# A hybrid decoder step on one core: score matmuls of the previous tile placed behind the second projection slab of a tile instead of behind the first

## The chip, the cores and the metric

The kernel runs on one core of one Trainium2 chip. The metric is the device time of one execution in microseconds (us), the median of several runs. Five engines run their own instruction streams side by side, each in its own order, and wait for each other by semaphores: TensorE (PE: matmuls and transposes), VectorE (DVE), ScalarE (ACT), GpSimd (POOL) and SyncE (SP), which here issues most of the DMA transfers. The profile gives waits of TensorE under the name of what released it.

## The reference

One layer of a decoder trunk is computed for a prompt of 2048 tokens and for 8 sample sequences of 4 tokens, with width 1024. Cut to what matters here:

```python
h = layer_norm(x) * (1 + scale(c)) + shift(c)          # adaLN: modulated by a vector c per sequence
z, xBC, dt, q, k, v = split(h @ w_in)                  # one combined projection
y_ssm = ssd_scan(silu(causal_conv(xBC)), dt, ...)      # Mamba-2 heads
q, k = rotary(q), rotary(k)                            # first quarter of each head of 64
y_att = softmax([q k^T / 8 in a window of 128, sink]) v   # 8 query heads, 2 key heads
x = layer_norm(alpha * x + gate * (concat(y_ssm, y_att) @ w_out))
x = layer_norm(alpha * x + gate * mlp(modulated x))    # squared ReLU, 4096 wide
```

Outputs are the two y, the convolution and SSM states, and the rotated keys and the values. The change lies in the part that makes q, k, v, dt and the attention of the prompt, all in float32 accuracy: each projection is done as three matmuls of split operands (high x high, high x low, low x high).

## The kernel before

The prompt is 16 tiles of 128 tokens; the 32 sample tokens are a 17th tile, NTILE, worked on after tile 8. The first stretch of the program ("sweep 1", up to about 395 us) loops over the tiles (L767 on). A second sweep for the other columns, the output projection and the MLP follow.

For a tile t the parts are: `st_x` loads x and makes its statistics on DVE (L189, L190) and normalises it (L321). `st_hT` transposes it on TensorE (L330, called xT below), modulates it (DVE L351, POOL L352) and splits it into high and low parts (ACT L171, POOL L172). `st_slab(t, n)` computes one half of 776 projected columns, 24 matmuls of 128x388 (L175 to L177) into one PSUM tile: slab 0 gives dt and most of q, slab 1 the rest of q, k and v. Slab 1 is copied out by ACT (L378, L379) and rotated by DVE (L385 to L388, from whose result kd, L413, is doubled). `st_qkT` transposes q and k (L418, L422) and splits them (qh and kTh on ACT, ql and kTl on DVE). `st_score` does 24 score matmuls (L440, two at a time on two halves of the rows), copies them out on ACT and DVE (L448, L449; the S copies) and runs softmax: maximum (L395), its scaled negative nm (L397), eight exponentials with a sum (L401), reciprocal (L404), and the division on POOL (L405). `st_PT` transposes the result (L464), copied by ACT (L465) and masked by DVE (PC, L467), and `st_PV` multiplies with v (L474), copied out as ao (L479).

In the first nine iterations an "extra" computes one chunk of the modulation for later layers: 8 matmuls (L267), a copy "part" on ACT (L270), one matmul that sums it (L272, the chunk's sum), and an addition on DVE (L274). The chunk's weights and bias are loaded by SP, and the load of a later x stands behind that of the bias in SP's order.

In the last iterations the weights of the second sweep are loaded and split: Wx, the pages pg, and at the end wzst (L634, 2 MB in two loads, into the buffer that tile 15's projection frees; eight splits on ACT with DVE and POOL). `decays_a` is a chain of small DVE operations on dt of all tiles (dkw, ea; L560 to L574).

The order of instructions on each engine isn't that of the source alone. A scheduler takes the source order and a model of its own of how long things take, and places each instruction; only SP's order is written out up to the tenth iteration. An explicit order without a semaphore ties the scores of a tile to a matmul of a projection slab: `mid`, the last matmul of the fourth of its eight steps (k == 3, L372, L373), which `st_score` hands to `side_by_side`, so that no score matmul is put ahead of it. PSUM tiles rotate over three buffers for mm (both slabs, one score tile in four, the chunk), two for tr (all transposes) and three for sc (the other score tiles and PV).

Of the kernel before, what the change touches and what calls it, by code (L numbers as in the profile page):

```python
# [119 lines left out]
def body(tc, I, O):  # L120
# [10 lines left out]
    def mm_tile():  # L131
        return ps.tile([128, 512], F32, tag="mm", name="mm", bufs=3)

    def tr_tile():
        return ps.tile([128, 512], F32, tag="tr", name="tr", bufs=2)
# [14 lines left out]
    def mm_dec(tmp, w, hs, wt):  # L150
        acc = mm_tile()
        for k in range(8):
            for l in range(2):
                PE.matmul(acc[:2 * ND, :w], lhsT=hs(k), rhs=wt(k, l), start=k + l == 0, stop=k + l == 8)
        S.activation(tmp[:2 * ND, :w], acc[:2 * ND, :w], AF.Copy)
        return tmp

    def sum2(out, tmp, w):
        PE.matmul(out[:ND, :w], lhsT=idt[:2 * ND, 192:224], rhs=tmp[:2 * ND, :w], start=True, stop=True)
# [14 lines left out]
    def mm3(out, ahi, alo, bhi, blo, first=True, last=True):  # L174
        PE.matmul(out, lhsT=ahi, rhs=bhi, start=first, stop=False)  # L175
        PE.matmul(out, lhsT=ahi, rhs=blo, start=False, stop=False)  # L176
        return PE.matmul(out, lhsT=alo, rhs=bhi, start=False, stop=last)  # L177
# [18 lines left out]
    def ptok(t):  # L196
        return 128 if t < NTILE else ND
# [114 lines left out]
    def st_x(t):  # L312
        P = ptok(t)
        x = xbuf()
        D.dma_start(out=x[:P], in_=I["x"][128 * t:128 * t + P])
        mv = p1.tile([128, 2], F32, tag="mv", name="mv", bufs=2)
        ln_stats(p1, x, P, mv)
        rs = rstd_of(p1, mv[:P, 1:2], P)
        V.tensor_copy(mean_all[:P, t, 0:1], mv[:P, 0:1])
        V.tensor_copy(mean_all[:P, t, 1:2], rs[:P])  # L320
        V.tensor_scalar(x[:P], x[:P], mv[:P, 0:1], rs[:P], ALU.subtract, ALU.mult)  # L321
        tl["x", t] = x
# [10 lines left out]
    def hT_store(t):  # L333
        hh = tl["hT", t]
        if t < NTILE:
            D.dma_start(out=hT_d[t], in_=hh.bitcast(F32))
        else:
            D.dma_start(out=hT_d[t][:, 0, :, :2 * ND], in_=hh[:, 0, :, :2 * ND].bitcast(F32))
# [17 lines left out]
    def st_slab(t, n):  # L356
        P = ptok(t)
        hh = tl["hT", t]
        if n == 0:
            tl["qkv", t] = p1.tile([128, 648], F32, tag="qkv", name="qkv", bufs=2)  # L360
            tl["v", t] = p1.tile([128, 128], F32, tag="v", name="v", bufs=5)
        qkv = tl["qkv", t]
        mm = tl.pop(("sm", t, n)) if t < 3 else mm_tile()
        sl = slice(388 * n, 388 * n + 388)
        if t == NTILE:
            tmp = mm_dec(p1.tile([128, 512], F32, tag="ao", name="tmp", bufs=2), 388, lambda k: hh[:, 0, k, :2 * ND],
                         lambda k, l: (W1l if l else W1h)[k][:, sl])
            sum2(mm, tmp, 388)
        elif t > 2:
            for k in range(8):  # L370
                ins = mm3(mm[:P, :388], hh[:, 0, k, :P], hh[:, 1, k, :P], W1h[k][:, sl], W1l[k][:, sl], k == 0, k == 7)
                if n == 0 and k == 3:  # L372
                    tl["mid"] = ins  # L373
        if n == 0:
            S.activation(qkv[:P, sl], mm[:P, :388], AF.Copy)
            V.tensor_copy(dt_all[:P, t, :], qkv[:P, 0:8])
            return
        S.activation(qkv[:P, 388:648], mm[:P, 0:260], AF.Copy)  # L378
        S.activation(tl["v", t][:P], mm[:P, 260:388], AF.Copy)  # L379
        qk = qkv[:P, 8:648].rearrange("p (h d) -> p h d", h=10)  # L380
        cos = cc(C_COS + 16 * t, 16)[:P].unsqueeze(1).to_broadcast([P, 10, 16])
        sin = cc(C_SIN + 16 * t, 16)[:P].unsqueeze(1).to_broadcast([P, 10, 16])
        t1 = p1.tile([128, 10, 16], F32, tag="rt1", name="rt1", bufs=1)
        t2 = p1.tile([128, 10, 16], F32, tag="rt2", name="rt2", bufs=1)
        V.tensor_tensor(t1[:P], qk[:, :, 0:16], cos, ALU.mult)  # L385
        V.tensor_tensor(t2[:P], qk[:, :, 0:16], sin, ALU.mult)
        V.tensor_tensor(qk[:, :, 0:8], t1[:P, :, 0:8], t2[:P, :, 8:16], ALU.add)
        V.tensor_tensor(qk[:, :, 8:16], t1[:P, :, 8:16], t2[:P, :, 0:8], ALU.add)  # L388
# [64 lines left out]
    def st_PT(t):  # L453
        Sx = tl.pop(("S", t))
        PT = p1.tile([128, 2, 512], F32, tag="PT", name="PT", bufs=1)
        v = tl["v", t]
        if t > 0:
            PC = p1.tile([128, 2, 512], F32, tag="PC", name="PC", bufs=1)
            vd = p1.tile([128, 128], F32, tag="vd", name="vd", bufs=2)
            V.tensor_tensor(vd, v, tl["v", t - 1], ALU.subtract)  # L460
        for g in range(2):
            tr = tr_tile()
            for r in range(4):
                PE.transpose(tr[:, 128 * r:128 * r + 128], Sx[:, 4 * g + r, :], ident)  # L464
            S.activation(PT[:, g, :], tr, AF.Copy)  # L465
            if t > 0:
                V.tensor_tensor(PC[:, g, :].rearrange("p (r n) -> p r n", r=4), tr.rearrange("p (r n) -> p r n", r=4),  # L467
                                le.unsqueeze(1).to_broadcast([128, 4, 128]), ALU.mult)
        tl["PT", t] = [(v, PT)] if t == 0 else [(tl["v", t - 1], PT), (vd, PC)]

    def st_PV(t):
        terms = tl.pop(("PT", t))
        o = sc_tile()
        side_by_side([lambda i=i, vv=vv, pt=pt, g=g: PE.matmul(  # L474
            o[64 * g:64 * g + 64, :], lhsT=vv[:, 64 * g:64 * g + 64], rhs=pt[:, g, :], start=i == 0,
            stop=i == len(terms) - 1, tile_position=(0, 64 * g))
            for i, (vv, pt) in enumerate(terms) for g in (1, 0)])
        ao = p1.tile([128, 4, 128], F32, tag="ao", name="ao", bufs=2)
        S.activation(ao.rearrange("p r n -> p (r n)"), o, AF.Copy)  # L479
        S.dma_start(out=att_d[t], in_=ao)  # L480
# [219 lines left out]
    n = len(seq)  # L700
# [66 lines left out]
    for i in range(n + 3):  # L767
        if i == 10:
            start.close()
        g = lambda j: seq[j] if 0 <= j < n else None  # L770
        t = g(i)
        if g(i + 5) is not None:
            st_x(g(i + 5))
        if i == 0:
            hT_store(2)
        elif i > 1 and g(i + 1) is not None:
            hT_store(g(i + 1))
        if t is not None:
            st_slab(t, 0)
        if g(i - 2) is not None and g(i - 2) < NTILE:  # L780
            st_PT(g(i - 2))
        if g(i - 1) is not None and g(i - 1) < NTILE:
            st_score(g(i - 1))
        if t is not None:
            st_slab(t, 1)
        if i >= 1 and extras:
            extras.pop(0)()
        if g(i - 2) is not None and g(i - 2) < NTILE:
            st_PV(g(i - 2))
        if t is not None and t < NTILE:  # L790
            st_qkT(t)
        if (i == 0 or i > 2) and g(i + 3 + 2 * (i == 0)) is not None:
            st_hT(g(i + 3 + 2 * (i == 0)))
        if t == NTILE:
            extras += [lambda: (dec_qT(), dec_score(0)), lambda: (dec_PT(0), dec_PV(0), dec_score(1)),
                       lambda: (dec_PT(1), dec_PV(1))]
        if i == 13:
            for j in range(2):
                w2_raw(j, wb0[:, j])
        if i == 14:  # L800
            for j in range(2):
                w2_raw(2 + j, hbuf[:, j])
        if i == 15:
            for j in range(2):
                w2_raw(6 + j, xb1[:, j])
            for k in range(2):
                w2_load(k)
            xq = pb.tile([128, 1024], F32, tag="xq", name="xq")
        if i == n - 1:
            ld_hT(0)  # L810
            for k in range(2, NA):
                w2_load(k)
            for j in range(2):
                w2_raw(4 + j, hbuf[:, j])
            decays_a()
            wz_raw()
        if i == n:
            for k in range(4, 8):
                w2_load(k)
            xproj(0, range(4))  # L820
            for k in range(4):
                wz_load(k)
        if i == n + 1:
            xproj(0, range(4, 8))
            for k in range(4, 8):
                wz_load(k)
            decays_b()
# [719 lines left out]
```

## Time and profile before

| what | value |
|---|---|
| median of 3 runs (lowest, highest) | 2451.91 us (2450.31, 2454.03) |
| the profiled execution | 2451.32 us, span 2449.5 us |
| TensorE busy | 2373.8 us, 97% of the span |
| DVE, ACT, POOL busy | 1445.4, 768.5, 859.9 us |
| mean granted TensorE clock | 0.989 |

The span runs from the first to the last instruction; 1.8 us of the execution lie outside. A row of a timeline has the start, the duration, the engine, the source line, the operation with the tiles it writes and reads, and in brackets the idle time ahead of it with the instruction that ended it. The line of a helper stands for all its callers (L171 and L172 for every split, L175 to L177 for every projection), so there the tile's name tells which it is: hb is the split input of sweep 1, hT that of the second sweep.

### The profile page before, as it was taken

What the parts mean: (1) busy time and instruction counts of PE and PEld (TensorE: products, weight loads), DVE (VectorE), ACT (ScalarE), POOL (GpSimd) and SP (SyncE); (2) the same over time, 40 slices, a digit from 0 to 9 for tenths busy, and PEclk for the clock granted to TensorE, in tenths of its full rate; (3) what the DMA queues carried; (4) which work ended last, traced back from release to release, by engine and by line L of the source; (5) the groups of instructions that cost most, each with busy time, mean ns of one, the idle gap of its engine ahead of it and who ended that gap; (6) DMA issues with size and microseconds to landing.
All of it is one profiled execution on the core that took longest, in us unless ns stands there. A gap on an engine that the chain in (4) does not pass through costs nothing.

```text
span 2449.5 us, 32265 instructions
## 1 busy us (share of the span) xinstructions
PE 2373.8 (97%) x12695; PEld 1987.6 (81%) x12695; DVE 1445.4 (59%) x2533; ACT 768.5 (31%) x1568; POOL 859.9 (35%) x587
## 2 busy tenths in 40 slices
PE   8899989999999999999999999999999999999997
PEld 6566769977997887887888888888889889889885
DVE  6766667877788766355454443448454554443448
ACT  3545554333343545412212212123312212212221
POOL 4333531233223223533323324337333323323335
PEclk9999999999999999999999999999999999999998
DMA  8755333223324356222112211117211211111111
GB/s 314 258 196 169 122 121 96 75 74 109 104 95 151 129 181 234 84 69 65 61 60 72 63 35 61 43 54 217 64 57 45 67 52 52 66 38 35 50 41 71
DMA packets 116104, 242.11 MB, mean 99 GB/s; under 512 B 26080, under 2 KB 61360, under 8 KB 112800
## 3 DMA queue, kind: packets, MB, share of 16 engines
q1 hardware_dynamic: 111552, 230.07, 28.1%
q10 hardware_dynamic: 4400, 9.98, 1.1%
q8 instruction: 100, 1.64, 0.3%
q14 instruction: 52, 0.43, 0.1%
HBM read 185.66 MB, written 55.37 MB: 98 GB/s over the span
## 4 chain that ended last, share of the span: by engine, by line
PE 80%; DVE 7%; ACT 1%; issue 1%; POOL 1%; DMA 1%; POOLq 0%; ACTq 0%; DVEq 0%; SPq 0%
PE sc L175 11%; PE sc L177 11%; PE sc L176 11%; PE mm L175 11%; PE mm L177 11%; PE mm L176 11%; PE tr L175 2%; PE tr L177 2%; PE tr L176 2%; DVE xc L667 1%; PE tr L1298 1%; PE sc L932 1%; PE sc L1129 1%; DVE nb L1325 0%; DVE p L1313 0%
## 5 line engine op out<-in xcount | busy, mean ns | idle before, releaser
L172 POOL TENSOR_TENSOR wdl<-st,wdh 128x1024 fp32r<-128x1024 f32 x63 | 154.6, 2455 | 480.7 <-ACT wdh L171 480.7
L1283 DVE TENSOR_TENSOR r<-r 128x320 f32<-128x320 f32 (+1 forms) x160 | 131.2, 820 | 303.0 <-ACT A L1279 103.1
L1313 DVE TENSOR_TENSOR p<-mm,p 128x512 f32<-128x512 f32 x278 | 187.8, 686 | 123.2 <-PE mm L177 123.2
L171 ACT ACTIVATE wdh<-st 128x1024 fp32r<-128x1024 f32 x63 | 66.9, 1061 | 557.1 <-PE mm L177 173.2
L175 PE MATMUL sc<-H,wvh 128*128 128x352 f32 (+1 forms) x640 | 225.7, 353 | 5.3 <-ACT r L1277 5.3
L176 PE MATMUL sc<-H,wvh 128*128 128x352 f32 (+1 forms) x640 | 226.0, 353 | 0.0
L177 PE MATMUL sc<-H,wvl 128*128 128x352 f32 (+1 forms) x640 | 225.7, 353 | 0.0
L175 PE MATMUL sc<-H,wuh 128*128 128x352 f32 (+1 forms) x640 | 223.8, 350 | 0.0
L177 PE MATMUL sc<-H,wul 128*128 128x352 f32 (+1 forms) x640 | 223.1, 349 | 0.0
L176 PE MATMUL sc<-H,wuh 128*128 128x352 f32 (+1 forms) x640 | 222.9, 348 | 0.0
L1277 ACT ACTIVATE r<-sc 128x352 f32<-128x352 f32 (+1 forms) x160 | 81.6, 511 | 291.7 <-PE sc L177 281.5
L1151 DVE TENSOR_TENSOR st<-st,gf 128x1024 f32<-128x1024 f32 x64 | 108.8, 1701 | 95.1 <-POOL wdl L172 65.7
L175 PEld LDWEIGHTS sc<-H,wvh 128*128 128x128 f32 x640 | 120.8, 189 | 18.1 <-ACT r L1277 5.7
L176 PEld LDWEIGHTS sc<-H,wvh 128*128 128x128 f32 x640 | 120.7, 189 | 12.3
L177 PEld LDWEIGHTS sc<-H,wvl 128*128 128x128 f32 x640 | 120.7, 189 | 11.9
L175 PEld LDWEIGHTS sc<-H,wuh 128*128 128x128 f32 x640 | 120.1, 188 | 11.1 <-ACT r L1277 0.8
L177 PEld LDWEIGHTS sc<-H,wul 128*128 128x128 f32 x640 | 120.5, 188 | 10.2
L176 PEld LDWEIGHTS sc<-H,wuh 128*128 128x128 f32 x640 | 120.2, 188 | 10.0
L183 POOL TENSOR_TENSOR rs<-ve,mhalf 128x1 f32<-128x1 f32 (+2 forms) x68 | 48.3, 710 | 210.2 <-DVE ve L182 187.9
L667 DVE SCALAR_TENSOR_TENSOR xc<-xq,cvw,xc 128x256 f32<-128x256 f32 x192 | 103.6, 543 | 3.3
L1282 DVE TENSOR_TENSOR ud<-r 128x32 f32<-128x32 f32 x32 | 48.2, 1506 | 92.2 <-ACT r L1277 92.2
L172 POOL TENSOR_TENSOR wvl<-st,wvh 128x1024 fp32r<-128x1024 f32 x32 | 77.1, 2410 | 63.9 <-ACT wvh L171 60.8
(496 smaller groups left out, 6521.0 us busy)
## 6 DMA issues: line engine op xcount, KB each, us to landing
st<-in_wd SPq DMA_DIRECT2D x64, 512.0 KB
st<-in_wu SPq DMA_DIRECT2D x63, 512.0 KB
wa<-in_w_ada SPq DMA_DIRECT2D x32, 512.0 KB
hT_d<-hb SPq DMA_DIRECT2D x16, 1024.0 KB
hT<-hT_d SPq DMA_DIRECT2D x16, 512.0 KB
hT<-hT_d SPq DMA_DIRECT2D x8, 1024.0 KB
csb<-cs_d SPq DMA_DIRECT2D x16, 512.0 KB
st<-xhat_d SPq DMA_DIRECT2D x16, 512.0 KB
```

What stands on the lines that cost most here:

```text
L171: S.activation(hi, src, AF.Copy)
L172: (eng or V).tensor_tensor(lo, src, hi.bitcast(F32), ALU.subtract)
L175: PE.matmul(out, lhsT=ahi, rhs=bhi, start=first, stop=False)
L176: PE.matmul(out, lhsT=ahi, rhs=blo, start=False, stop=False)
L177: return PE.matmul(out, lhsT=alo, rhs=bhi, start=False, stop=last)
L183: G.tensor_tensor(r[:P], v[:P], mhalf[:P, 0:n], ALU.pow)
L667: V.scalar_tensor_tensor(dst_, src(j), cvw[:, f, j:j + 1], dst_, ALU.mult, ALU.add)
L1151: V.tensor_tensor(st, raw, scale, ALU.mult)
L1277: S.activation(r[:, :n], mm[:, :n], AF.Relu)
L1282: V.tensor_tensor(ud, r[:, w:n], r[:, w:n], ALU.mult)
L1283: V.tensor_tensor(r[:, :w], r[:, :w], r[:, :w], ALU.mult)
L1313: V.tensor_tensor(acc[t][:, sl], mm, acc[t][:, sl], ALU.add)
```

## The change

The anchor `mid` moves from the first slab to the second, and in the loop the second slab of a tile comes ahead of the scores of the tile before.

```diff
@@ -369,7 +369,7 @@
         elif t > 2:
             for k in range(8):
                 ins = mm3(mm[:P, :388], hh[:, 0, k, :P], hh[:, 1, k, :P], W1h[k][:, sl], W1l[k][:, sl], k == 0, k == 7)
-                if n == 0 and k == 3:
+                if n == 1 and k == 3:
                     tl["mid"] = ins
         if n == 0:
             S.activation(qkv[:P, sl], mm[:P, :388], AF.Copy)
@@ -779,10 +779,10 @@
             st_slab(t, 0)
         if g(i - 2) is not None and g(i - 2) < NTILE:
             st_PT(g(i - 2))
+        if t is not None:
+            st_slab(t, 1)
         if g(i - 1) is not None and g(i - 1) < NTILE:
             st_score(g(i - 1))
-        if t is not None:
-            st_slab(t, 1)
         if i >= 1 and extras:
             extras.pop(0)()
         if g(i - 2) is not None and g(i - 2) < NTILE:
```

The instructions stay the same in number and size. On every engine the order is unchanged up to the first slab of tile 3 (about 90 us) and from the second sweep's projections on (about 395 us). In between it is new; three places show it.

TensorE at tile 6, before (146 to 166 us in the profile; the first row is the end of slab 0, the L175 and L177 rows behind it are the begin and end of slab 1):

```order
L177 MATMUL mm<-pg_128,hb_104 128x388
L330 MATMUL tr<-idt,hbuf 128x128 x4
L440 MATMUL sc<-kTh,qh 128x256
L330 MATMUL tr<-idt,hbuf 128x128 x4
...
L440 MATMUL sc<-kTh,ql 128x256
L175 MATMUL mm<-pg_121,hb_104 128x388
...
L464 MATMUL tr<-idt,S 128x128 x4
...
L177 MATMUL mm<-pg_128,hb_104 128x388
L267 MATMUL mm<-wa,scT 32x512 x8
L474 MATMUL sc<-PT,v 64x512 x2
L474 MATMUL sc<-PC,vd 64x512 x2
L272 MATMUL mm<-part,idt 9x512
```

and in the change, from the xT transposes inside slab 0 on:

```order
L330 MATMUL tr<-idt,hbuf 128x128 x8
...
L464 MATMUL tr<-idt,S 128x128 x8
...
L177 MATMUL mm<-pg_128,hb_104 128x388
L440 MATMUL sc<-kTh,qh 128x256 x2
...
L440 MATMUL sc<-kTh,ql 128x256
L267 MATMUL mm<-wa,scT 32x512 x8
L418 MATMUL tr<-idt,qkv 128x128 x4
L422 MATMUL tr<-idt,kd 128x128 x2
L474 MATMUL sc<-PT,v 64x512 x2
L474 MATMUL sc<-PC,vd 64x512 x2
L272 MATMUL mm<-part,idt 9x512
```

The scores of tile 5 now follow slab 1 of tile 6 in one run, the transposes of softmax (of tile 4) stand together inside slab 1, and q and k of tile 6 are transposed ahead of the chunk's sum.

ScalarE at the same tile, before:

```order
L448 ACTIVATE S<-sc 128x256
L171 ACTIVATE hb_101<-hbuf 128x512
L465 ACTIVATE PT<-tr 128x512 x2
L401 ACTIVATE S,su<-S,nm 128x128
L399 ACTIVATE ex<-ex 128x8
L401 ACTIVATE S,su<-S,nm 128x128 x7
L378 ACTIVATE qkv<-mm 128x260
L379 ACTIVATE v<-mm 128x128
L270 ACTIVATE part<-mm 128x512
```

and in the change:

```order
L465 ACTIVATE PT<-tr 128x512 x2
L378 ACTIVATE qkv<-mm 128x260
L379 ACTIVATE v<-mm 128x128
L448 ACTIVATE S<-sc 128x256 x2
L448 ACTIVATE S<-mm 128x256
L448 ACTIVATE S<-sc 128x256
L270 ACTIVATE part<-mm 128x512
L171 ACTIVATE qh<-tr 128x512
L171 ACTIVATE kTh<-tr 128x2x128
L401 ACTIVATE S,su<-S,nm 128x128
```

Part, qh and kTh have moved from behind the eight exponentials to ahead of them.

ScalarE at the end of the stretch, where tile 15 is done (pg_4130 to pg_4309 are the eight wzst pages), before:

```order
L562 ACTIVATE dkw_3871<-dkw_3871 128x136
L171 ACTIVATE pg_4130<-wzst 128x512
L401 ACTIVATE S,su<-S,nm 128x128
L399 ACTIVATE ex<-ex 128x8
L401 ACTIVATE S,su<-S,nm 128x128 x7
L171 ACTIVATE qh<-tr 128x512
L171 ACTIVATE kTh<-tr 128x2x128
L171 ACTIVATE pg_4133<-wzst 128x512
```

and in the change:

```order
L171 ACTIVATE pg_4130<-wzst 128x512
...
L171 ACTIVATE pg_4309<-wzst 128x512
L171 ACTIVATE qh<-tr 128x512
L479 ACTIVATE ao<-sc 128x512
L561 ACTIVATE dkw_3871<-dt_all 128x136
L171 ACTIVATE kTh<-tr 128x2x128
L480 DMA att_d<-ao 128x512
L562 ACTIVATE dkw_3871<-dkw_3871 128x136
L401 ACTIVATE S,su<-S,nm 128x128
```

All eight splits of wzst now stand ahead of qh and kTh of tile 15, and the exponentials (of tile 14) behind them.

## The prediction, made before the result was known

> **What bounds the kernel now.** I read the page first, then the waits of TensorE between 60 and 400 us (the only stretch in which the order differs), then the timeline around each long wait.
>
> ```profile
> span 2449.5 us, 32265 instructions
> PE 2373.8 (97%) x12695; PEld 1987.6 (81%) x12695; DVE 1445.4 (59%) x2533; ACT 768.5 (31%) x1568; POOL 859.9 (35%) x587
> ```
>
> TensorE is busy for 2373.8 of 2449.5 us. The change adds and removes no matmul, so it can win or lose only a part of the 75.7 us in which TensorE stands idle, the matmuls slowed by a lower clock behind such an idle, and the switches between kinds of matmul. The profiled execution took 2451.32 us, 1.8 more than its span and 0.6 below the median of the three runs (2451.91). I sum against 2451.3.
>
> ```profile
> PE sc L440 <- ACT kTh L171: 12.3, 9, 4.1
> PE tr L330 <- DVE mv L190: 5.9, 1, 5.9
> ```
>
> These rows give the waiting matmul, what released it, the total, the count and the longest. The 5.9 lies in the first tiles, whose order stays. The other large ones are single waits, and the timeline shows their places:
>
> ```profile
> 105.63 1.08 PE L474 MATMUL sc<-PT,v 128*64 128x512 f32 x4 [1.43 <-ACT PT L465]
> ...
> 165.26 1.03 PE L272 MATMUL mm<-part,idt 128*9 128x512 f32 x2 [2.49 <-ACT part L270]
> 166.21 0.52 PE L175 MATMUL mm<-pg,hb 128*128 128x388 f32 x1
> ...
> 169.77 0.40 PE L177 MATMUL mm<-pg,hb 128*128 128x388 f32 x1
> ```
>
> Behind the 2.49 us wait slab matmuls start 0.32 us apart up to 169.77. Undisturbed they start 0.18 apart:
>
> ```profile
> 107.87 0.34 PE L176 MATMUL mm<-pg,hb 128*128 128x388 f32 x1
> 108.05 0.34 PE L177 MATMUL mm<-pg,hb 128*128 128x388 f32 x1
> ```
>
> From 166.21 to 169.77 there are eleven intervals, so the low clock cost (0.32 - 0.18) x 11, about 1.6 us on top of the wait. The 1.43 us wait had no such tail: 107.87 to 108.05 lies 2.2 us behind its end and is at full speed. So the wait at 165.26 costs 2.49 + 1.6 = 4.1.
>
> The Trainium skill ("TensorE: Matmul & The Clock Gate", Part 1) says that the clock falls to half after at least one idle window of about 3.4 us. Here it fell after 2.49, so the trace disagrees on the length; by the page alone the gain at this place would be 2.5, and the sum below 1.6 smaller.
>
> **The change part by part.** First the tiles with modulation chunks (88 to 215 us). What held TensorE at 165.26 stands on ScalarE:
>
> ```profile
> 161.01 0.40 ACT L401 ACTIVATE S<-S,nm 128x128 f32<-128x128 f32 x1 [2.71 <-DVE nm L397]
> ...
> 164.62 0.58 ACT L270 ACTIVATE part<-mm 128x512 f32<-128x512 f32 x1
> ```
>
> The eight exponentials begin after a wait of 2.71 for the row maximum, and the copy "part" that TensorE wants starts 3.6 us later, queued behind them, L378 and L379. In the changed order ScalarE has L378, L379, the S copies, part, qh, kTh and only then the exponentials. So this wait goes: -4.1. The 1.43 at 105.63 is a PV waiting for PT copies that stood among the S copies; now PT sits inside the second slab, with the rest of that slab, all scores and a chunk ahead of PV: -1.4.
>
> What the new order takes away is cover. Softmax of a tile used to run beside a second slab more; now from the last score matmul to the PT transposes of that tile TensorE has only: chunk, PV, qT and kT, the chunk's sum, slab 0, eight xT transposes, half of slab 1.
>
> ```profile
> 158.98 1.92 PE L267 MATMUL mm<-wa,scT 128*32 128x512 f32 x16
> 160.83 1.08 PE L474 MATMUL sc<-PT,v 128*64 128x512 f32 x4
> ...
> 357.99 1.03 PE L464 MATMUL tr<-idt,S 128*128 128x128 f32 x8
> 358.95 0.39 PE L440 MATMUL sc<-kTl,qh 64*128 64x256 f32 x2
> ```
>
> Chunk 1.85 (158.98 to 160.83), PV 1.9 (160.83 to 162.77, where the wait of 2.49 begins), eight transposes 0.96 (357.99 to 358.95), so six for qT and kT 0.7, chunk sum 0.95 (165.26 to 166.21), slab 0 24 x 0.178 = 4.3, xT 0.96, half a slab 2.1: 12.8 us. The softmax chain before:
>
> ```profile
> 140.71 0.17 DVE L397 TENSOR_SCALAR nm<-mx 128x8 f32<-128x8 f32 x1
> ...
> 160.82 0.15 DVE L397 TENSOR_SCALAR nm<-mx 128x8 f32<-128x8 f32 x1
> ...
> 136.36 0.28 PE L440 MATMUL sc<-kTh,ql 64*128 64x256 f32 x1
> ...
> 145.24 1.90 POOL L405 TENSOR_TENSOR S<-S,su 128x1024 f32<-128x1024 f32 x1 [5.21 <-DVE su L404]
> ...
> 146.24 0.44 PE L175 MATMUL mm<-pg,hb 128*128 128x388 f32 x1
> ...
> 153.31 0.28 PE L440 MATMUL sc<-kTl,qh 64*128 64x256 f32 x1
> ...
> 153.43 0.28 PE L440 MATMUL sc<-kTh,ql 64*128 64x256 f32 x1
> 153.64 0.44 PE L175 MATMUL mm<-pg,hb 128*128 128x388 f32 x1
> ...
> 164.87 2.04 POOL L405 TENSOR_TENSOR S<-S,su 128x1024 f32<-128x1024 f32 x1 [5.20 <-DVE su L404]
> ```
>
> From the last score matmul (136.64, 153.71) to the end of L405 (147.14, 166.91) it took 10.5 us for one tile and 13.2 for the next; the longer one lost its time ahead of the negated maximum (160.82 is 7.1 behind the last score, 140.71 only 4.1), where DVE had a PC product and the normalising of x in between. In the new DVE order those stand ahead of the S copies, so I take the shorter end, 10.5: 2.3 us to spare, cost nothing. The other end is 0.4 late per tile, 6 tiles, 2.4.
>
> The second cover is for x. Its load lands late, and DVE's statistics wait for it in order:
>
> ```profile
> 152.50 0.69 DVE L189 BATCH_NORM_STATS2 bst<-xb 128x6 f32<-128x512 f32 x1 [4.84 <-DMA xb<-in_x]
> ...
> 173.63 1.28 DVE L189 BATCH_NORM_STATS2 bst<-x 128x6 f32<-128x512 f32 x2 [5.35 <-DMA x<-in_x]
> ```
> ```profile
> L467 DVE TENSOR_TENSOR PC<-tr,cst 128x512 f32<-128x512 f32 x26 | 17.2, 680 | 6.5 <-ACT PT L465 6.5
> ...
> L385 DVE TENSOR_TENSOR rt<-qkv,c 128x160 f32<-128x160 f32 (+1 forms) x17 | 7.4, 435 | 5.5 <-ACT qkv L378 5.5
> ...
> L321 DVE TENSOR_SCALAR xb<-xb,mv,rs 128x1024 f32<-128x1024 f32 x6 | 5.3, 886 | 0.0
> ```
>
> The second x starts 7.4 us behind its slab 0 (166.21); the first 6.3 behind its own (146.24). In the new order PC and the rotary products of slab 1, which qT needs, are queued on DVE behind these statistics. Statistics 1.3, small steps of the variance 1.5 (an estimate), normalising 0.9, two PC products 1.4, four rotary products of at most 0.43, 1.7: x + 6.8, so 13.1 to 14.2 us behind slab 0's start. TensorE comes to qT after slab 0, xT, slab 1, PT, 24 scores and the chunk. A pair of scores starts 0.12 behind the last (153.31, 153.43) and the switch adds 0.1, so 24 take at least 1.5; I take 1.7. Then 4.3 + 1.0 + 4.3 + 1.0 + 1.7 + 1.9 = 14.2. It fits with 0 to 1.1 to spare; I take nothing. An x that lands 2 us later would cost some 1 to 2 per tile.
>
> Switches: in the tile shown in the order, xT no longer splits the scores and the two PT groups are one, three switches fewer of about 0.1 us (scores start 0.12 apart, the first slab matmul, at 153.64, 0.21 behind the last of them); over six tiles -1 to -2, taken -1.
>
> **Late tiles (260 to 345 us).** The score matmuls of a tile stand one slab further back, yet the first four are again put right behind the kT transposes in most tiles:
>
> ```profile
> 301.20 0.58 PE L440 MATMUL sc<-kTh,qh 64*128 64x256 f32 x2 [3.62 <-ACT kTh L171]
> ...
> 320.24 0.39 PE L440 MATMUL sc<-kTh,qh 64*128 64x256 f32 x2 [0.74 <-ACT kTh L171]
> ...
> 335.38 0.39 PE L440 MATMUL sc<-kTh,qh 64*128 64x256 f32 x2 [0.80 <-ACT kTh L171]
> ```
>
> The 3.62 is tile 12; kTh there queues behind eight exponentials of tile 11, which wait for DVE's splits of weights, and the new order has the same sequence: stays. For tiles 13 and 14 eight or more slab matmuls come between kT and score now: -1.5.
>
> **The end of the stretch.** Take T0 as the end of slab 1 of tile 15 (342.8, when the load into the buffer it frees is issued).
>
> ```profile
> 342.82 0.92 SPq L634 DMA_DIRECT2D wzst<-in_wz  x2
> ...
> 348.31 0.63 ACT L171 ACTIVATE pg<-wzst 128x512 fp32r<-128x512 f32 x1 [2.13 <-DMA wzst<-in_wz]
> ...
> 352.76 3.74 ACT L171 ACTIVATE pg<-wzst 128x512 fp32r<-128x512 f32 x7
> ...
> 352.92 0.58 PE L440 MATMUL sc<-kTh,qh 64*128 64x256 f32 x2 [4.07 <-ACT kTh L171]
> ...
> 365.35 1.08 PE L474 MATMUL sc<-PT,v 128*64 128x512 f32 x4 [2.27 <-DVE S L449]
> ...
> 374.78 0.38 PE L175 MATMUL mm<-hT,Wx 128*128 128x256 f32 x1 [0.90 <-ACT xq L688]
> ```
>
> Before, kTh of tile 15 stood behind one of the eight splits of wzst; now it stands behind all eight, and these wait for the load that slab 1 releases. The first half landed 5.5 us behind T0; I put the second at 9.5 (seven splits from 352.76 ran without a wait), four splits of 0.53 behind it, then qh, ao, an Abs and kTh, 1.8 together: score 15 at new T0 + 13.4. But scores and PT of the tiles ahead, 2.7 us (1.7 and 1.0), now lie behind T0, so T0 comes 2.7 sooner: old T0 + 10.7, against 352.92, T0 + 10.1, in the old order. So +0.6. The waits of 2.27 and 0.90 come from DVE's chain of decays colliding with PC and the copies; in the new order more matmuls of the next projection stand ahead of PV of tile 14, and I count both as gone, so -2.6 together. Bounds: -4 if kTh is no later, +6 if the loads land 3 later and the 2.27 grows with them.
>
> **Sum.** -4.1 - 1.4 - 1 - 1.5 - 2.6 = -10.6. Some waits will arise at the new places, as the small ones of 0.7 and 0.8 above do in the old order; I leave 2 us for three of them: -8.6, so 2442.7 for a profiled execution and 2443 as the median. This case's own range is 2438 to 2447.
>
> **The rivals.**
> - A, slower: x lands 2 to 3 us later than I put it, and DVE holds PC and rotary behind its statistics; qT waits in each of six tiles 1.5 to 2.5 us, some with a low clock behind them (1.6). It decides once x is more than 7.4 us behind slab 0. For it: two waits of about 5 us are there now, both for x. Against it: the load goes out when DVE has read the chunk's sum, and in the new order nothing that waits long stands ahead of that read. Price 6 x 2 + 3 x 1.6 = 17, less the 10.6: 2458.
> - B, no change: the tail takes it back. All eight splits ahead of kTh cost the +6 above in place of -2.6, so the sum is -2 + 2: 2451. For it: ScalarE's fixed order with a 2 MB load in front. Against it: the 2.7 us by which the load is issued sooner.
> - C, the change does less than it says: scores still directly behind kT in late tiles, and the wait for part replaced by one for kTh or PT of similar length: only switches and one wait go, -3: 2449.
> - D, more: the 3.62 at tile 12 and a low clock behind it like the 1.6 above go too: 2443 - 5.2 = 2438.
>
> **How the numbers follow.** My forecast 0.50, A 0.17, B 0.12, C 0.13, D 0.08. 0.2% (4.9 us) is about what a measurement of this kernel can tell from no change. Faster: forecast and D, 0.58. Same: B and C, 0.25. Slower: A, 0.17. The range 2436 to 2457 leaves out most of A and the low end of D.
>
> **What would show it.** Right: no wait of L272 for part and no low clock between 160 and 170 us; scores of the early tiles as 24 in one run with no wait for kTh; L464 and L418 without waits. Wrong: L418 waiting for L388 or L464 for L405 in tile after tile (A, or the chain of 13.2), the last kTh wait above 8 us followed by waits of L474 (B), or waits of 2 us and more still in the early tiles (C).

## The result, and the profile after

The changed kernel takes 2438.74 us (median; 2437.16 to 2440.59), the kernel before 2451.11 in the same runs: a ratio of 0.9946, with a 95% interval of 0.9935 to 0.9958. That is 12.4 us faster, where 8.6 were forecast (2443, range 2436 to 2457). The profiled execution has a span of 2438.8 us.

The page after, to be read beside the two rows of the page before:

```profile
span 2438.8 us, 32262 instructions
PE 2371.9 (97%) x12695; PEld 1986.1 (81%) x12695; DVE 1463.0 (60%) x2533; ACT 769.9 (32%) x1568; POOL 856.8 (35%) x587
```

TensorE is busy 1.9 us less and the span is 10.7 shorter. From 60 us, ahead of the first difference in order, to the same matmul of the second sweep (at 382.77 before, 370.18 after) it is 12.6 us shorter: 9.8 of idle time and 2.8 of busy time. The other 1.9 this one execution lost behind that point, where the order is the same. The waits of TensorE between 60 and 400 us, after:

```profile
PE sc L440 <- ACT kTh L171: 6.6, 7, 2.4
PE sc L474 <- DVE S L449: 6.3, 1, 6.3
PE tr L330 <- DVE mv L190: 5.5, 1, 5.5
PE sc L440 <- ACT ao L479: 1.2, 1, 1.2
PE tr L418 <- DVE qkv L388: 1.0, 1, 1.0
PE tr L418 <- DVE PC L467: 0.9, 1, 0.9
```

The rows for part and for PT are gone, kTh has gone from 12.3 to 6.6, and the wait for a score copy has grown from 2.3 to 6.3 and stands at another tile. Where the time went, in three stretches:

Early tiles. From the chunk's sum of tile 3 to that of tile 8 (five tiles), first before, then after:

```profile
106.64 1.03 PE L272 MATMUL mm<-part,idt 128*9 128x512 f32 x2
...
204.77 1.03 PE L272 MATMUL mm<-part,idt 128*9 128x512 f32 x2
```

```profile
107.16 1.03 PE L272 MATMUL mm<-part,idt 128*9 128x512 f32 x2
...
196.03 1.03 PE L272 MATMUL mm<-part,idt 128*9 128x512 f32 x2
```

98.1 us before, 88.9 after. Of the 9.2, the wait for part is 2.5, the low clock behind it 1.6 (the granted clock was 0.55 from 166.21 to 170), and half a PV that lies inside the boundary only before 0.9. The wait of 1.43 for PT lies just ahead of the first row and is gone too. There remain 4.2 us that are neither wait nor clock. The same matmuls run in fewer visits: TensorE changes 52 times between kinds that use the array differently (matmuls on the whole array and transposes, scores on 64 rows, PV, the chunk, its sum) before and 35 times after. Ten of the 17 changes saved are to or from the scores: TensorE comes to them 12 times before and 7 times after.

Late tiles. The wait of tile 12 for kTh is 3.62 before and 2.42 after, those of 0.74 and 0.80 are gone, and so are three of 1.26, 0.69 and 0.47 in the part of the sample tokens (the decode part). Not all of this is gain. From the chunk's sum of tile 8 to the second sweep, with the end of the stretch, it takes 178.0 us before and 174.2 after: idle time falls from 18.9 to 13.5, but busy time rises from 159.2 to 160.7, and TensorE comes to the scores 20 times in place of 18. Two visits at the 0.4 measured below would be 0.8 of that; where the rest arose is open.

The end of the stretch. Here a new wait took the place of the old ones. One of the old ones that the prediction does not show, before:

```profile
347.31 1.11 PE L418 MATMUL tr<-idt,qkv 128*128 128x128 f32 x4 [2.49 <-DVE qkv L388]
```

TensorE, then DVE, after:

```profile
336.46 1.98 PE L474 MATMUL sc<-PT,v 128*64 128x512 f32 x4 [6.34 <-DVE S L449]
...
343.51 0.58 PE L440 MATMUL sc<-kTh,qh 64*128 64x256 f32 x2 [0.56 <-ACT kTh L171]
```

```profile
327.48 2.58 DVE L172 TENSOR_TENSOR pg<-hbuf,pg 128x1024 fp32r<-128x1024 f32 x1 [0.54 <-ACT pg L171]
329.98 3.36 DVE L172 TENSOR_TENSOR pg<-xb,pg 128x1024 fp32r<-128x1024 f32 x1
333.26 1.39 DVE L385 TENSOR_TENSOR rt<-qkv,c 128x160 f32<-128x160 f32 x1
334.57 1.38 DVE L386 TENSOR_TENSOR rt<-qkv,c 128x160 f32<-128x160 f32 x1
335.88 0.77 DVE L449 COPY_PREDICATED S<-c,sc 128x256 f32<-128x256 uint32 x2
```

PV of tile 13 needs one of the three sc buffers, all held by the scores of tile 14, and DVE comes to copy them out only at 335.88, behind two weight splits and two rotary products. The kTh wait I had put at the end of that tail is 0.56, since PV's wait ran beside it. Waits of the tail add up to 9.7 before (2.49, 4.07, 2.27, 0.90) and 9.0 after (1.20, 6.34, 0.88, 0.56).

### The profile page after: what moved, and what is told of

Its sections match the earlier page's. It is cut to its first block, busy times and chain, and to the rows that moved or that the text cites. A ratio compares the mean times of both kernels' runs of the same rounds, so it can differ in the third digit from the quotient of the medians.

```text
span 2438.8 us, 32262 instructions
## 1 busy us (share of the span) xinstructions
PE 2371.9 (97%) x12695; PEld 1986.1 (81%) x12695; DVE 1463.0 (60%) x2533; ACT 769.9 (32%) x1568; POOL 856.8 (35%) x587
## 4 chain that ended last, share of the span: by engine, by line
PE 50%; DVE 2%; DMA 1%; issue 0%; ACT 0%; SPq 0%; POOL 0%; POOLq 0%; DVEq 0%; ACTq 0%
PE sc L175 10%; PE sc L177 10%; PE sc L176 10%; PE mm L175 5%; PE mm L177 5%; PE mm L176 5%; PE tr L175 1%; PE tr L177 1%; PE tr L176 1%; PE tr L1298 1%; DVE nb L1325 1%; DVE p L1332 1%; DVE p L1313 0%; DMA H<-h_d 0%; SPq L1465 0%
## 5 line engine op out<-in xcount | busy, mean ns | idle before, releaser
L175 PE MATMUL sc<-H,wvh 128*128 128x352 f32 (+1 forms) x640 | 226.2, 353 | 5.2 <-ACT r L1277 5.2
L177 PE MATMUL sc<-H,wvl 128*128 128x352 f32 (+1 forms) x640 | 226.1, 353 | 0.0
L175 PE MATMUL sc<-H,wuh 128*128 128x352 f32 (+1 forms) x640 | 223.8, 350 | 0.0
L177 PE MATMUL sc<-H,wul 128*128 128x352 f32 (+1 forms) x640 | 223.1, 349 | 0.0
L175 PEld LDWEIGHTS sc<-H,wvh 128*128 128x128 f32 x640 | 121.1, 189 | 18.1 <-ACT r L1277 5.7
L176 PEld LDWEIGHTS sc<-H,wvh 128*128 128x128 f32 x640 | 121.1, 189 | 12.4
L177 PEld LDWEIGHTS sc<-H,wvl 128*128 128x128 f32 x640 | 121.0, 189 | 11.9
L175 PEld LDWEIGHTS sc<-H,wuh 128*128 128x128 f32 x640 | 120.1, 188 | 11.1 <-ACT r L1277 0.8
L177 PEld LDWEIGHTS sc<-H,wul 128*128 128x128 f32 x640 | 120.5, 188 | 10.2
```

## The experiments

The change has two parts. The anchor alone alters no row of any engine's order, and the loop's order alone gives the changed kernel's rows on every engine. So the anchor does nothing by itself here, and only the loop's order had to be taken apart. Where an edit picks tiles, it is this:

```diff
-                if n == 1 and k == 3:
+                if n == (CONDITION) and k == 3:
...
+        slab1 = lambda: t is not None and st_slab(t, 1)
+        score = lambda: g(i - 1) is not None and g(i - 1) < NTILE and st_score(g(i - 1))
+        for part in ((slab1, score) if t is None or (CONDITION) else (score, slab1)):
+            part()
```

### Early tiles alone, late tiles alone

`e1_early` has the condition t <= 8 or t == NTILE, `e2_late` 8 < t < NTILE.

> Slab 1 goes ahead of the scores, with its anchor, only for tiles up to 8 and the sample tile; later tiles keep the old order. Theory of the prediction: almost all of the gain is in the tiles with modulation chunks (the wait for part, the one for PT, one low clock, switches), so this alone gives some 9 to 12 of the 12.4 us: 2439 to 2442 where before is 2451. Theory from comparing the two traces: waits there fell by 3.4 us, the low clock by 1.6 and interruptions of slabs cost 1 to 2 less, so 6 to 7 us here: 2444 to 2445, and the rest belongs to later tiles.

> The complement: slab 1 ahead of the scores only for tiles 9 to 15. Theory of the prediction: late tiles -1.5, tail -2.6, so 2447. Theory from the traces: waits from 215 us to the tail fell by 5, the low clock behind the wait of tile 12 by 2 and the tail by 0.7, so 5 to 6 us of gain or more: 2445. If the two parts don't add up to the whole, the gain is not local and something carries over (the place of the x loads, the buffers).

Early: 2444.06 us (before 2452.4), ratio 0.9962 [0.9949, 0.9974]. Late: 2451.17, ratio 0.9993 [0.9984, 1.0002], an interval that holds 1, so no gain is shown. The product, 0.9955, lies within the interval of the whole change (0.9935 to 0.9958): the two add up as far as can be told. Most of the gain is early, some 8 to 9 us, between what the two theories had there; the 5 to 6 expected of the late tiles did not come by themselves.

The trace of the second has the old early order, and with it the wait for part:

```profile
166.85 1.03 PE L272 MATMUL mm<-part,idt 128*9 128x512 f32 x2 [2.69 <-ACT part L270]
167.81 0.44 PE L175 MATMUL mm<-pg,hb 128*128 128x388 f32 x1
168.09 0.34 PE L176 MATMUL mm<-pg,hb 128*128 128x388 f32 x1
168.27 0.34 PE L177 MATMUL mm<-pg,hb 128*128 128x388 f32 x1
```

A longer wait, 2.69, and no low clock behind it: matmuls start 0.18 apart from 168.09 on. The 1.6 us that I had added to the 2.49 belong to one execution and do not follow from a wait of that length. The remainder of 4.2 does not hang on that execution: the same five tiles take 97.0 us in this trace, and 96.2 in the trace of the kernel before with its splits on DVE (below; a wait of 1.92, no low clock). Less the wait for part and the half PV, each is 4.5 us longer than after the change.

### The change without its last iteration

Condition t != 15.

> The change without its last iteration: for tile 15 the scores of tile 14 stay ahead of slab 1. In the changed kernel PV of tile 13 waits 6.3 us for a copy of the scores of tile 14 on DVE. Theory 1, the new wait comes from what the change does to the last iteration: it goes here, but the old tail (waits of 2.5, 4.1, 2.3 and 0.9) comes back: within 2 us of the changed kernel, 2437 to 2441. Theory 2, the tail was a gain by itself: 3 us or more slower than the changed kernel, 2442 or more.

2443.81 us, ratio 0.9962 [0.9949, 0.9976], 5 us above the median of the changed kernel and, by the ratios to the kernel before, 4: theory 2, but the two intervals overlap. The wait of 6.3 is gone as theory 1 had it, but three others stand there:

```profile
332.07 1.98 PE L474 MATMUL sc<-PT,v 128*64 128x512 f32 x4 [2.66 <-ACT PT L465]
...
339.38 1.98 PE L474 MATMUL sc<-PC,vd 128*64 128x512 f32 x4 [5.34 <-DVE PC L467]
...
345.47 0.58 PE L440 MATMUL sc<-kTh,qh 64*128 64x256 f32 x2 [2.63 <-ACT kTh L171]
```

They add up to 10.6, more than the 9.0 of the changed kernel's tail. So the long wait after the change isn't the price of the last swap: a long one for DVE (5.34) stands there either way.

### Why DVE is late at the end

The changed kernel, with GpSimd doing none of the last splits (the fourth run):

```diff
-        split(Wx[k][0], Wx[k][1], raws.pop(k), V if k % 2 else G)
+        split(Wx[k][0], Wx[k][1], raws.pop(k), V if k % 2 or k >= NA else G)
...
-        split(Wz[k][0], Wz[k][1], raws.pop(("z", k)), V if k % 2 else G)
+        split(Wz[k][0], Wz[k][1], raws.pop(("z", k)))
```

> The changed kernel with the low parts of the last weight splits (Wx from 4 on, all wzst) computed on DVE alone, so that GpSimd does none of them: DVE gets 2 more of 1.2 and 4 more of 0.7, 5 us of work more at the undisturbed durations. Theory 1, DVE is late in the tail because GpSimd works beside it (its splits took 2.6 and 3.4 us there against 1.2 undisturbed, the rotary products 1.4 against 0.3): DVE gets through the same queue sooner, the wait of 6.3 falls to 2 to 4 and the time by 2 to 4, 2435 to 2437. Theory 2, DVE is late because of the number of instructions queued ahead of the score copies: the wait stays at 6 or grows, 2439 to 2441.

2436.62 us, ratio 0.9933 [0.9921, 0.9946]: the two faster than the changed kernel that theory 1 expected, though the time alone does not show it, as the two intervals overlap. The trace does. DVE, then TensorE:

```profile
323.46 1.22 DVE L172 TENSOR_TENSOR pg<-hbuf,pg 128x1024 fp32r<-128x1024 f32 x1
...
332.76 0.31 DVE L385 TENSOR_TENSOR rt<-qkv,c 128x160 f32<-128x160 f32 x1
333.00 0.31 DVE L386 TENSOR_TENSOR rt<-qkv,c 128x160 f32<-128x160 f32 x1
333.24 0.76 DVE L449 COPY_PREDICATED S<-c,sc 128x256 f32<-128x256 uint32 x2
```

```profile
333.81 1.50 PE L474 MATMUL sc<-PT,v 128*64 128x512 f32 x4 [2.04 <-DVE S L449]
```

The same split takes 1.22 in place of 2.58, a rotary product 0.31 in place of 1.39, and the wait falls from 6.34 to 2.04, with more instructions in DVE's queue. Some of that comes back: the waits of the tail are 0.68, 2.04, 0.37, 1.14 and 1.51, 5.7 in place of 9.0. What held DVE stands beside it on GpSimd. In the changed kernel:

```profile
327.08 1.90 POOL L405 TENSOR_TENSOR S<-S,su 128x1024 f32<-128x1024 f32 x1 [4.23 <-DVE su L404]
328.95 3.31 POOL L172 TENSOR_TENSOR pg<-xb,pg 128x1024 fp32r<-128x1024 f32 x1
```

and in the fourth run, where one split of DVE still meets the division of softmax:

```profile
328.73 1.90 POOL L405 TENSOR_TENSOR S<-S,su 128x1024 f32<-128x1024 f32 x1 [14.10 <-ACT ao L479]
329.58 2.12 DVE L172 TENSOR_TENSOR pg<-xb,pg 128x1024 fp32r<-128x1024 f32 x1 [1.03 <-ACT pg L171]
```

All three slow splits of DVE (2.58, 3.36, 2.12) end 1.08 us behind the end of the instruction beside them on GpSimd, about as long as a split takes alone. They look as if they had stood until GpSimd was done. DVE was late because GpSimd worked beside it. The Trainium skill ("SBUF — State Buffer", in its part on the two sides of the memory) says that a DVE operation with two SBUF inputs and a GpSimd operation that reads SBUF share one pair of ports, which one of them holds for a whole instruction while the other blocks; splits and rotary products have two inputs, and the trace agrees.

The same edit in the kernel before:

> The kernel before, with the same edit as the fourth run (the last weight splits' low parts on DVE alone). Theory 1, DVE beside GpSimd is slow in this stretch whatever the order of the scores: the splits take 1.2 and 0.7 us here too, the waits of 2.5 for qkv and 2.3 for the copies shrink, 2448 to 2450. Theory 2, it is the new order that brings the splits of both engines together ahead of PV: the time stays at 2451 to 2453, since the 4.1 for kTh is set by ScalarE.

2452.65 us beside 2452.94, ratio 0.9998 [0.9989, 1.0006]: theory 2. The waits of 2.27 and 0.90 went, as theory 1 had it, but the one for kTh, which ScalarE sets, grew from 4.07 to 5.78: the edit moved ScalarE's order too, and four splits of wzst stand ahead of the exponentials there in place of one. So this run doesn't show what DVE's speed alone is worth in the old order.

The changed kernel with all splits on DVE (`V if k % 2 else G` left out in both lines):

> The fourth run's kernel with the first four splits of Wx on DVE too. Around 285 us two of them ran beside GpSimd's (2.6 and 2.2 us on DVE, 2.4 and 3.4 on GpSimd) ahead of the copies of the scores of tile 11, and tile 12 waits 2.4 us for kTh behind the exponentials. Theory 1, contention: four at 1.2 us take DVE about as long as two did, 4.9 against 4.8, but GpSimd is free for the rest, so the wait of tile 12 stays within 1 of 2.4 and the time within 1 of the fourth run's 2436.6. Theory 2, the number of DVE instructions decides: the wait grows by 2.4 and the time by 2 to 4.

2435.75 us, ratio 0.9934 [0.9921, 0.9948]: within 1 of the fourth run, and tile 12 waits 2.40 (for ql on DVE in place of kTh), both as theory 1 has it. The fourth run's kernel with a part of the next projection moved forward:

```diff
+            for k in range(4, 8):
+                w2_load(k)
             wz_raw()
+            xproj(0, range(1))
         if i == n:
-            for k in range(4, 8):
-                w2_load(k)
-            xproj(0, range(4))
+            xproj(0, range(1, 4))
```

> The fourth run's kernel with the first 24 matmuls of the next projection, and the four weight splits they need, written one iteration sooner, so that they stand among the last scores and ahead of PV of tile 13. Theory 1, in the tail TensorE is idle for want of matmuls that are ready, and 24 of 0.12 us cover up to 2.8 us of the 5.5 us of waits: 2 to 3 us faster than the fourth run, 2434. Theory 2, they wait in their new place for pages that DVE has yet to split, and hold the scores behind them: as slow as the fourth run or slower, 2437 to 2440.

2438.3 us, from 2433.6 to 2441.4, ratio 0.994 [0.9927, 0.9954]. It can't be told from the changed kernel or from the fourth run; neither theory is settled.

### Is it the wait for part?

The kernel before, with one line changed:

```diff
-        S.activation(part, acc, AF.Copy)
+        V.tensor_copy(part, acc)
```

> The kernel before, with one edit: the copy part (L270) is made by DVE in place of ScalarE, so it no longer stands behind the exponentials; the score matmuls stay where they were. Theory 1, the early gain of the change is the wait for part and the low clock behind it: this alone gives 2.5 to 4 us, 2447 to 2450 where before is 2452, and no wait of the chunk's sum is left. Theory 2, the early gain is the run of uninterrupted slabs and scores: the wait goes or moves to another matmul and the time stays, 2451 to 2453.

2456.47 us, ratio 1.0016 [1.0008, 1.0025]: slower than before. The wait of 2.49 is gone, and these stand in the early tiles in its place:

```profile
106.58 1.02 PE L272 MATMUL mm<-part,idt 128*9 128x512 f32 x2 [1.05 <-DVE part L270]
...
170.37 0.66 PE L418 MATMUL tr<-idt,qkv 128*128 128x128 f32 x4 [0.64 <-DVE qkv L388]
178.00 0.76 PE L330 MATMUL tr<-idt,hbuf 32*128 32x32 f32 x8 [1.31 <-DVE ql L172]
185.86 1.08 PE L474 MATMUL sc<-PC,vd 128*64 128x512 f32 x4 [1.06 <-DVE PC L467]
206.63 0.63 PE L418 MATMUL tr<-idt,qkv 128*128 128x128 f32 x4 [1.27 <-DVE qkv L388]
```

5.3 us of waits in place of the 3.9 for PT and part, 1.4 of the 3.5 by which the kernel is slower; where the rest arose I did not find. The copy left ScalarE's queue and joined DVE's, which has its own consumers; the new order instead put a stretch of both slabs ahead of everything that has to come back from the two engines.

### What a change of kind costs

What was left in the early tiles, 4.2 us for 17 fewer changes of kind, gives 0.25 us each. Two kernels add changes to the changed kernel and no work. In the first two runs the eight PT transposes are cut into pieces inside slab 1 of tiles 3 to 8 (after steps 1, 3, 5, 6, or after every step), by orders without semaphores (shortened; the anchor `mid` moves to the last step as well):

```diff
             for k in range(8):
                 ins = mm3(mm[:P, :388], ...)
+                if last is not None:
+                    follow(first matmul of this step, last)
+                if n == 1 and k in STEPS and "pt" in tl:
+                    last = next(tl["pt"])     # a piece of st_PT, behind ins
```

> The changed kernel once more, beside the next two on the same chip: 2437 to 2441.

> The changed kernel with the eight PT transposes of a tile set inside slab 1 as four pieces of two (after its steps 1, 3, 5 and 6), for tiles 3 to 8, by orders without semaphores; the scores stay behind slab 1. Same instructions, 32 more changes of kind on TensorE (109 for 77 in these six tiles). Theory 1, a change of kind costs 0.23 us (the old order has 118 up to the sample tile's q transposes, the new one 100, and what is neither wait nor low clock fell by 4.2): 7 us slower than the changed kernel, 2446. Theory 2, changes are nearly free and the early gain is only waits and the clock: within 2 of the changed kernel.

> The same with eight pieces of one transpose, after every step: 74 more changes of kind (151 for 77). Theory 1: 74 x 0.23 = 17 us slower than the changed kernel, 2456, slower than before the change too. Theory 2: within 2 of the changed kernel. If the cost is per transposed piece but smaller (0.1 on entry, nothing on exit) it is 4 to 8 us, 2443 to 2447.

The changed kernel beside them 2440.39, four pieces 2446.52, eight pieces 2447.12 (ratios to before 0.9947 [0.9935, 0.996], 0.9973 [0.9963, 0.9983], 0.9973 [0.9962, 0.9985]). Four pieces seem to bear out theory 1, with 6 for the 7 expected, but eight should then cost 17 and cost 7. The trace has the reason. Pieces of one transposition, in the run with eight:

```profile
156.99 0.34 PE L184 MATMUL mm<-pg,hb 128*128 128x388 f32 x1
157.16 0.27 PE L479 MATMUL tr<-idt,S 128*128 128x128 f32 x1
157.19 0.42 PE L182 MATMUL mm<-pg,hb 128*128 128x388 f32 x1
157.45 0.34 PE L183 MATMUL mm<-pg,hb 128*128 128x388 f32 x1
```

The piece takes 0.03 and the slab matmul behind it 0.26 in place of 0.18: 0.11 in all, what a transposition costs in a row of eight. So a piece is free. What both kernels lost is a wait, in the run with eight at tile 3:

```profile
101.17 0.47 PE L479 MATMUL tr<-idt,S 128*128 128x128 f32 x1 [5.43 <-POOL S L420]
```

5.4 here and 4.4 in the other, where the first piece was tied to the first steps of slab 1 and softmax of the tile wasn't done (L420 is L405 of the other kernels); with a second wait for the same, both have 5.7 to 5.9 us of it in all, and behind the first one the granted clock was 0.50 for 4 us, 1.7 us more. From the chunk's sum of tile 3 on, the five tiles take 89.0 us in both, as against 88.9 in the changed kernel. Theory 1 falls in its general form: changes between matmuls and transposes of the whole array cost nothing.

The other kind of change is to the scores. The last kernel cuts the 24 scores into four pieces behind steps 1, 3, 5 and 7 of slab 1 (shortened):

```diff
-            side_by_side([... for jj in range(2) for i in range(3) for par in (1, 0)], mid)
+            calls = [... for jj in range(2) for i in range(3) for par in (1, 0)]
+            for q in range(2):
+                yield side_by_side(calls[6 * q:6 * q + 6], tl.pop("mid", None))
```

> The changed kernel with the scores of tiles 2 to 7 split into four pieces of six matmuls, set behind steps 1, 3, 5 and 7 of slab 1 of the next tile by orders without semaphores; xT and PT fall between score matmuls too. Same instructions; TensorE comes to the scores 33 times in place of 9 in these six tiles. Theory 1: what the early tiles gained beyond waits and clock is fewer visits to the scores (in the old order a slab or xT stands between them), some 0.3 to 0.4 us per visit for both ends, where pieces of PT in a slab cost next to nothing: 24 x 0.35 = 8 us slower than the changed kernel, 2448, with few new waits in the early tiles. Theory 2: visits are free as well, and what is left over in the comparison of the two traces is work that lies on other sides of the boundary: within 2 us of the changed kernel, 2438 to 2442, or slower by new waits alone.

2448.29 us, ratio 0.9984 [0.9975, 0.9993], beside 2448 expected: theory 1. There is no wait of TensorE in its tiles 3 to 8. One visit:

```profile
158.30 0.34 PE L178 MATMUL mm<-pg,hb 128*128 128x388 f32 x1
158.47 0.34 PE L179 MATMUL mm<-pg,hb 128*128 128x388 f32 x1
158.75 0.39 PE L449 MATMUL sc<-kTh,qh 64*128 64x256 f32 x2
158.97 0.28 PE L449 MATMUL sc<-kTl,qh 64*128 64x256 f32 x2
159.09 0.28 PE L449 MATMUL sc<-kTh,ql 64*128 64x256 f32 x2
159.30 0.44 PE L177 MATMUL mm<-pg,hb 128*128 128x388 f32 x1
159.58 0.34 PE L178 MATMUL mm<-pg,hb 128*128 128x388 f32 x1
```

Four intervals are 0.1 too long: 0.28 ahead of the first pair (0.17 or 0.18 else), 0.22 behind it (0.12 else), 0.21 behind the last pair, 0.28 behind the first slab matmul. That is 0.4 for a visit, 0.2 for a change of kind. Five tiles of this kernel:

```profile
108.30 1.03 PE L274 MATMUL mm<-part,idt 128*9 128x512 f32 x2
...
206.75 1.03 PE L274 MATMUL mm<-part,idt 128*9 128x512 f32 x2
```

98.5 us in place of 88.9, with 1.4 of it for half a PV and four transposes more inside the boundary: 8.2 us for 45 more changes (80 for 35), 0.18 each. At 0.2 each the 17 changes that the new order saves are worth 3.4 of the 4.2. Seven of them are between PV, the chunk, its sum and the whole array; the last chunk or PV matmul ahead of another kind takes 0.52 in place of 0.43 in these traces, but no run varies those changes alone. The Trainium skill ("TensorEngine Tiling (Array Packing)", Key Properties) says that a change of the tiling mode, and not of the tile alone, drains the array. The traces agree: scores on 64 rows pay on both sides, transposes of the whole array don't. I hadn't weighed it in the prediction; it speaks for the change.

## Why the prediction was right, and where it was off

**Bound and direction** held: the work is the same, and what changed is idle time, clock and changes of kind in the stretch from 90 to 390 us.

**The waits for part and PT (-4.1 and -1.4)** went, as the order on ScalarE had said, and only one grew in the early tiles, for kTh (0.96 at 201.42, where 0.40 stood before). But the sum held 1.6 for the low clock as if it followed from the wait; the run with a wait of 2.69 and no low clock shows that it doesn't. That the profiled execution before had it was luck. And the wait alone was no handle: with part on another engine the time got longer.

**The covers** (softmax with 0.4 missing to 2.3 to spare, x with 0 to 1.1) were enough: no wait of L464 or L418 stands in the changed kernel between 100 and 330 us. Rival A did not come. The runs with PT tied to the first steps of slab 1 show how near it was for the first tiles: 4.4 and 5.4 us of wait at tile 3.

**Switches (-1)** is the term that was mis-sized: what is neither wait nor clock measured -4.2. The count was about right, three per tile forecast and 17 in five tiles found, though in two of these tiles transposes of softmax still split the scores. The price was not: 0.1 taken from one interval (153.43 to 153.64), and then the lower end of the sum. A change costs about 0.2, because the neighbours pay as well; the row at 153.64 shows it, with 0.44 for a slab matmul that takes 0.34 elsewhere. Only changes to another use of the array count: the two groups of PT that became one were worth nothing.

**Late tiles (-1.5).** The two waits went. The 3.62 at tile 12, taken to stay, is 2.42, and the low clock behind it is gone in this profile (but not in the other one of the changed kernel, see the end). Busy time grew at the same time, and the change for tiles 9 to 15 alone is worth 1 to 2 us with an interval that holds zero, so that part is not settled. Rival D's 2438 is where the time came out, but not for its reason: the 3.62 gave 1.2, and the gain lies early.

**The tail (-2.6)** was wrong in its steps. Neither the eight splits of wzst on ScalarE nor the decays set it, but DVE beside GpSimd, ahead of the copies that free the sc buffers; kTh of tile 15 was waited for 0.56 only. The waits gave back 0.7 and no more. Rival B's sign was wrong, its thought that the tail makes a new wait was not.

**The 2 us left for new waits** were too many outside the tail, where kTh grew by 0.6. The sum was 3.8 us short: 3.2 of it is the switches, -4.2 where -1 stood, and the other errors (the low clock, the late tiles, the tail, the new waits) go both ways and are not settled one by one.

## What to carry to other kernels

Count how often TensorE changes between matmuls that use the array differently, and not only its idle time: a visit to half-array matmuls cost 0.4 us here and is in no list of waits. A wait that was taken away by moving the late copy to another engine came back there (3.9 us became 5.3); the same wait did not come back where more independent work was put ahead of its consumer. Before a late engine is given less to do, look at the durations of its instructions beside those of its neighbour.

## What the hardware showed that I had not expected

The clock fell behind an idle of only 0.41 us. After:

```profile
255.61 0.65 PE L440 MATMUL sc<-kTh,qh 64*128 64x256 f32 x2 [0.41 <-ACT kTh L171]
...
257.04 0.53 PE L176 MATMUL mm<-pg,hb 128*128 128x388 f32 x1
257.36 0.53 PE L177 MATMUL mm<-pg,hb 128*128 128x388 f32 x1
...
259.52 0.34 PE L175 MATMUL mm<-pg,hb 128*128 128x388 f32 x1
```

Slab matmuls start 0.32 apart from 257.04 on for 2.3 us (granted clock 0.52 from 256.5 to 259.5), behind a wait of 0.41, after some five us of transposes and small matmuls of the decode part. The second profile of the changed kernel, with the same order, has it the other way round: full clock there, and 0.50 for 5.6 us behind the wait of 2.42 at tile 12, where the first has none. Elsewhere a wait of 2.49 had a low clock behind it in one execution and 2.69 none in another. The Trainium skill ("TensorE: Matmul & The Clock Gate", Part 1) has the clock decided by windows of 3.4 us that run freely; the scatter agrees with that, the length of the idle that the Trainium skill asks for there does not.
